# Late operands in their order of use, a pinned sum, and first loads behind a store, in a one-core encoder layer

## The chip, the cores and the metric

The kernel runs on one core of one Trainium2 chip. The metric is device time in microseconds (us): the median of several executions, with the lowest and the highest beside it. One more execution is taken with the hardware profiler; its page and its trace are what the views below show. Their times are microseconds from the start of its span.

The engines are called by their names in the profile: PE (TensorE, matmuls), ACT (ScalarE), DVE (VectorE), POOL (GpSimd) and SP (SyncE, which here only issues DMAs). An engine works through its own queue in order; a waiting instruction holds everything behind it.

## The reference, cut to what matters

One layer over 1024 positions with a width of 1024, all in f32:

```python
h = x
hn = rmsnorm(h, norm_mix_g)
z = hn @ w_in                       # pooling mixer and chunked attention
h = h + concat([pool_mixer(u), chunk_attention(q, k, v)]) @ w_out
hn = rmsnorm(h, norm_ffn_g)
up = hn @ w_up                      # 1024 -> 2 * 2816
gt, val = up[..., :2816], up[..., 2816:]
gt = causal_dwconv(gt, conv_w, conv_b)          # width 3 along the positions
h = h + (gelu(gt) * val) @ w_down   # the second projection, 2816 -> 1024
hn = rmsnorm(h, norm_ple_g)
gate = sigmoid(hn @ w_ple_gate + b_ple_gate)
h = h + gate * (p @ w_ple)          # p: 256 wide per position
return rmsnorm(h, final_g)
```

The change lies in the gated MLP (`w_up`, `w_down`) and in the passage to the embedding projection (`p @ w_ple`).

## The kernel before

**Split matmuls.** Every f32 operand is split into a high part (ACT rounds it, L133) and a low part (DVE subtracts, L134); the helper is `split`. `mm3` multiplies two split operands with three matmuls (L128 to L130). Where an operand is to be negated, ACT does so at L990 and DVE at L991.

**First projection.** The 2816 columns are 22 tiles `fi` of 128. Each tile is computed with seven products, numbered 1 to 7, after the manner of a fast 2x2 block scheme; `steps` gives their order, for tiles from 2 on (1, 5, 6, 2, 7, 3, 4). `up(fi, ...)` runs them. A product is 12 matmuls. Its weights are sums of blocks of `w_up`, which SP loads into a ring of six buffers `rawu` (`fetch`, L699), DVE adds (`summed`, L703) and `split` splits. Small steps take the results up: L788, L792 (ACT), L811, L812, L819, L822, L828 (DVE); the convolution and the GELU are L837 to L840; L854, L856 and L847 multiply gate and value.

**Second projection.** The results of tiles 0 to 19 are stored to DRAM (`Yd`, L898) and used in five groups of four tiles, again with seven products per group, here in the order (1, 2, 5, 4, 6, 7, 3) (`DOWN_ORDER`). They are called product 1 to 7 below, the ones of the first projection up products. Each is 24 matmuls and four additions to the result (`down_next`, L1008), placed between the up products of a later tile (`downs`, `places`). Its operands are sums of blocks of `w_down` and `Yd`: `ask` issues the first block's load on SP (L956) and the further ones as accumulating DMAs on POOL (L954) into the raw buffers `RW`. `split_next` splits them into four pairs, three of them in the tile `BQ`. In the last group product 4's activation operand is formed in part by DVE: at L986 it adds the buffer "grow", which holds product 5's operand, to the buffer "one".

**The end.** Tiles 20 and 21 do not go through DRAM. Their `w_down` blocks, the embedding `pT` and its weights `w_ple` are the late operands: twelve pieces, loaded on SP (L1068) into free `rawu` buffers named in `late` and split by `late_pairs`, in the order of `pieces`. Then come the embedding projection (`ple_mm`, 48 matmuls for the first half), the second projection of tiles 20 and 21 (`down_mm`), the gate and the last norm.

**What sets the order.** PE's order is that of the program (a manual schedule). The other engines' queues are set out at build time by a scheduler by priority, except for instructions marked with `keep_in_program_order` or `issue_after`. The marked ones of before are the twelve late pairs, the first split of the second projection and its first loads:

```python
def late_pairs(n):
    for _ in range(n):
        src, hi, lo = pieces[npiece[0]]
        t = late[npiece[0]]
        npiece[0] += 1
        sp.dma_start(t, src)
        split(t, hi, lo, True)
```

Of the kernel before, what the change touches and what calls it, by code (L numbers as in the profile page):

```python
# [9 lines left out]
ALU = mybir.AluOpType  # L10
# [83 lines left out]
def trunk(tc, xT, pT, vecs, w_qk0, w_in, w_v, bias, counts, pool_w, w_out, w_up, w_down,  # L94
          w_gate, w_ple, out):
    nc = tc.nc
    act, dve, pe, pool, sp = nc.scalar, nc.vector, nc.tensor, nc.gpsimd, nc.sync

    with tc.tile_pool(name="sb", bufs=1) as sb, \
# [20 lines left out]
        def f(kb, n):  # L120
            return F[:, int(kb * KW):int(kb * KW) + n]
# [206 lines left out]
        def keys(i):  # L328
            t = i % NTOK
            k0 = max(0, t - 4)  # L330
            return i // NTOK, t, k0, t + 1 - k0
# [209 lines left out]
        for i in range(NI + 3):  # L541
            if i < NI:
                h, t, k0, nk = keys(i)
# [40 lines left out]
        HS = [slice(0, 512), slice(512, 1024)]  # L584
# [3 lines left out]
        Yb = f(52.25, 1024)  # L588
# [82 lines left out]
        rawu = [f(2 * s, 512) for s in range(4)] + [f(40, 512), f(42, 512)]  # L671
# [83 lines left out]
        for z, d in enumerate((0, 4, 1, 5, 2, 6, 3, 7)):  # L755
            k = z // 2
# [33 lines left out]
        def seed(to, bank, scale=1.0):  # L790
            with tc.high_priority(AHEAD):
                act.activation(PS[:, to], PS[:, bank], AF.Copy, scale=scale)  # L792
# [34 lines left out]
        def gate0(bank):  # L827
            dve.tensor_tensor(Gb[:, 2:2 + 512], PS[:, bank], rst[:, HS[0]], ALU.mult)  # L828
# [13 lines left out]
        def values_in(ts, negative=None):  # L842
            b = max(ts.start, 512)
            if ts.stop > b:
                dve.tensor_tensor(V[:, b:ts.stop], V[:, b:ts.stop], rst[:, b:ts.stop], ALU.mult)
            if negative is None:
                dve.tensor_tensor(Yb[:, ts], Yb[:, ts], V[:, ts], ALU.mult)  # L847
                return
            for h in range(2):
                if HS[h].stop <= ts.start or HS[h].start >= ts.stop:  # L850
                    continue
                y = Yb[:, HS[h]]
                if h == negative:
                    dve.scalar_tensor_tensor(y, y, -1.0, V[:, HS[h]], ALU.mult, ALU.mult)  # L854
                else:
                    dve.tensor_tensor(y, y, V[:, HS[h]], ALU.mult)  # L856

        def store(dst, ts=slice(0, SEQ)):
            split(Yb[:, ts], dst[:, ts], dst[:, 1024 + ts.start:1024 + ts.stop])
# [13 lines left out]
        Yd = {fi: dp.tile([P, SEQ], F32, name=f"Yd{fi}") for fi in range(NF - 2)}  # L873
# [9 lines left out]
        def up(fi, dst, hooks=None):  # L883
            if fi == 0:
                pool.memset(Gb[:, 0:2], 0.0)
                gate0(firsts[0][0])
            if fi == 1:
                seed(firsts[1][1], firsts[1][0], -1.0)
            for n in steps[fi]:
                step(fi, n)  # L890
                for hook in (hooks or {}).get(n, ()):
                    hook()
            if isinstance(dst, int):

                for part in [HS[0:1], HS[1:2]] if fi == NF - 3 else [HS]:
                    values_in(slice(part[0].start, part[-1].stop), dst)
                    for ts in part:
                        sp.dma_start(Yd[fi][:, ts], Yb[:, ts])  # L898
                        stored.add((fi, HS.index(ts)))
                    ask()  # L900
                if fi > 3:
                    split_next()
                return
            for ts in HS if fi % 2 else [slice(0, SEQ)]:
                values_in(ts)
                if dst is not None:
                    store(dst, ts)

        stored = set()
        raws, pairs = {}, {}  # L910
        split_done, asked = set(), set()

# [18 lines left out]
        def buffer(side, n):  # L931
            return "grow" if n in (5, 6, 3) else "one"

        def ask(pinned=False):

            if not raws:
                return
            for side in "wa":
                for kind in ("one", "grow"):
                    queue = todo_of[side, kind]  # L940
                    while queue:
                        g, n, before = queue[0]
                        if before is not None and (side,) + before not in split_done:
                            break
                        if side == "a" and not all((group_of(g)[2 * k + j], t) in stored for k, t in parts(side, g, n)[0] for j in range(2)):
                            break
                        queue.pop(0)
                        asked.add((side, g, n))
                        grown = parts(side, g, n)[1]
                        for j, srcs in sources(side, g, n):  # L950
                            t = raws[side, kind, j]
                            for z, src in enumerate(srcs):
                                if z or grown:
                                    pool.dma_start(t, src, accum_op=ALU.add)  # L954
                                else:
                                    i = sp.dma_start(t, src)  # L956
                                    if pinned:
                                        tc.keep_in_program_order(i)

        todo_of = {}  # L960
        for side in "wa":
# [11 lines left out]
        def split_next(pinned=False):  # L973
            if nsplit[0] == len(sequence) or nsplit[0] > ndown[0]:
                return
            g, n = sequence[nsplit[0]]
            if not all((side, g, n) in asked for side in "wa"):
                return
            nsplit[0] += 1
            for side in "wa":  # L980
                sign = -1.0 if side == "a" and n in NEGATIVE else 1.0
                for j in range(2):
                    t = raws[side, buffer(side, n), j]
                    hi, lo = pairs[side, j]
                    if (side, g, n) == ("a", 4, 4):
                        dve.tensor_tensor(t, t, raws["a", "grow", j], ALU.add)  # L986
                    if sign > 0:
                        split(t, hi, lo, pinned)
                    else:
                        act.activation(hi, t, AF.Copy, scale=-1.0)  # L990
                        dve.scalar_tensor_tensor(lo, t, -1.0, rv(hi), ALU.mult, ALU.subtract)  # L991
                split_done.add((side, g, n))
            ask()
# [24 lines left out]
        for fi in range(4):  # L1018
            up(fi, negative(fi))
            if fi == 1:  # L1020
                b_pool = tc.tile_pool(name="bq", bufs=1)
                bp = b_pool.__enter__()
                B = bp.tile([P, 3072], F32R, name="BQ")
                RW = bp.tile([P, 4096], F32, name="RW")
                spots = [B[:, 1024 * z:1024 * (z + 1)] for z in range(3)] + [r(60, 1024)]
                for s, side in enumerate("wa"):
                    for j in range(2):
                        p_ = spots[2 * s + j]
                        pairs[side, j] = p_[:, 0:512], p_[:, 512:1024]
                        for q, kind in enumerate(("one", "grow")):  # L1030
                            z = 4 * s + 2 * q + j
                            raws[side, kind, j] = RW[:, 512 * z:512 * (z + 1)]
                ask(True)
            if fi == 2:
                for d in range(4):
                    for a, b, op in ((H[4 + d][:, HS[0]], H[4 + d][:, HS[1]], ALU.subtract),
                                     (H[d][:, HS[1]], H[4 + d][:, HS[1]], ALU.add)):
                        dve.tensor_tensor(a, a, b, op)
                ask()
                split_next(True)  # L1040
# [8 lines left out]
        wp = [(r(44 + 8 * k, 1024), r(48 + 8 * k, 1024)) for k in range(2)]  # L1049
        pt = [[(r(b, 512), r(b + 2, 512)) for b in (96 + 16 * h, 104 + 16 * h)] for h in range(2)]  # L1050
        banks = (4, 5, 6, 7, 0, 2, 1, 3)
        nl = len(loads)
        late = [rawu[(nl + z) % 6] for z in (0, 1, 5, 3, 2, 0, 1, 5, 3, 4, 2, 0)]
        pieces = []
        for z, fi in enumerate(last_f):
            pieces += [(w_down[fi, :, ts], wd2[z][0][:, ts], wd2[z][1][:, ts]) for ts in HS]
        pieces += [(pT[k, :, HS[0]], *pt[0][k]) for k in range(2)]
        for k in range(2):
            pieces += [(w_ple[k, :, ts], wp[k][0][:, ts], wp[k][1][:, ts]) for ts in HS]
        pieces += [(pT[k, :, HS[1]], *pt[1][k]) for k in range(2)]  # L1060
        npiece = [0]

# [8 lines left out]
        up(last_f[0], None, downs(last_f[0], (3, 5)))  # L1071
        hooks = downs(last_f[1], (0, 2, 4, 6))
        hooks.setdefault(1, []).insert(0, lambda: store(gv2[0]))
        for n, many in ((5, 2), (6, 4), (7, 4), (4, 2)):
            hooks.setdefault(n, []).insert(0, lambda many=many: late_pairs(many))
        up(last_f[1], gv2[1], hooks)
        b_pool.__exit__(None, None, None)
# [211 lines left out]
```

## Time and profile before

| what | before |
|---|---|
| median of 3 executions | 1149.34 us (1148.21 to 1151.45) |
| profiled execution | 1145.45 us |
| its span, first to last instruction | 1143.7 us |
| PE busy | 1127.9 us (99%) |
| DVE busy | 889.5 us (78%) |
| ACT busy | 604.6 us (53%) |
| POOL busy | 142.9 us (12%) |
| mean granted clock of PE | 0.996 |
| HBM read, written | 109.13 MB, 14.68 MB |

How to read the rows below: a timeline row gives start, duration, engine, line and operation, output and input, and, in brackets, how long the engine stood idle before it and what ended that. A row of the waits gives the waiting group, what released it, the total, how often, and the longest. A row of the chain of waits gives start, duration and what ran. A row of a window gives its length and, for PE, PEld, DVE, ACT and POOL, busy time and number of instructions, then the granted clock, the DMA share and GB/s. A row of DMA issues gives the median time from issue to landing at its end. PE matmuls overlap: what counts is from start to start, 0.227 us for one of 128x512 at full clock.

### The profile page before, as it was taken

What the parts mean: (1) busy time and instruction counts of PE and PEld (TensorE: products, weight loads), DVE (VectorE), ACT (ScalarE), POOL (GpSimd) and SP (SyncE); (2) the same over time, 40 slices, a digit from 0 to 9 for tenths busy, and PEclk for the clock granted to TensorE, in tenths of its full rate; (3) what the DMA queues carried; (4) which work ended last, traced back from release to release, by engine and by line L of the source; (5) the groups of instructions that cost most, each with busy time, mean ns of one, the idle gap of its engine ahead of it and who ended that gap; (6) DMA issues with size and microseconds to landing.
All of it is one profiled execution on the core that took longest, in us unless ns stands there. A gap on an engine that the chain in (4) does not pass through costs nothing.

```text
span 1143.7 us, 15749 instructions
## 1 busy us (share of the span) xinstructions
PE 1127.9 (99%) x5675; PEld 956.1 (84%) x5675; DVE 889.5 (78%) x1546; ACT 604.6 (53%) x1071; POOL 142.9 (12%) x188
## 2 busy tenths in 40 slices
PE   9999999999999999999999999999999999999997
PEld 7988998888888878888888888888888878788897
DVE  7678878879658788878788778877878779886864
ACT  8568677765655544434353435343534444574644
POOL 0000000073002200120112011201120112000000
PEclk9999999999999999999999999999999999999999
DMA  7110102104500244575558455745574547320012
GB/s 265 38 49 31 50 12 68 40 28 147 176 19 10 76 128 138 142 172 139 156 144 179 130 156 148 170 134 152 146 177 133 146 131 158 118 93 19 1 75 74
DMA packets 64446, 124.84 MB, mean 109 GB/s; under 512 B 7280, under 2 KB 8560, under 8 KB 64368
## 3 DMA queue, kind: packets, MB, share of 16 engines
q1 hardware_dynamic: 50400, 98.60, 25.4%
q0 software_dynamic: 13824, 25.17, 13.6%
q8 instruction: 44, 0.72, 0.3%
q14 instruction: 34, 0.28, 0.1%
q10 hardware_dynamic: 144, 0.07, 0.0%
HBM read 109.13 MB, written 14.68 MB: 108 GB/s over the span
## 4 chain that ended last, share of the span: by engine, by line
PE 88%; DVE 4%; issue 2%; ACT 2%; DMA 1%; POOL 1%; SPq 0%; DVEq 0%; POOLq 0%; ACTq 0%
PE PS L129 27%; PE PS L128 27%; PE PS L130 27%; PE PS L370 2%; DVE R L134 2%; PE PS L388 1%; PE PS L387 1%; PE PS L345 1%; PE PS L344 1%; ACT R L133 1%; DMA F<-in_w_down 1%; DMA F<-in_w_up 0%; DMA F<-in_w_qk 0%; PE PS L353 0%; PE PS L352 0%
## 5 line engine op out<-in xcount | busy, mean ns | idle before, releaser
L128 PE MATMUL PS<-R 128*128 128x512 f32 (+1 forms) x1176 | 442.2, 376 | 2.9 <-ACT PS L792 2.2
L130 PE MATMUL PS<-R 128*128 128x512 f32 (+1 forms) x1176 | 437.6, 372 | 0.0
L129 PE MATMUL PS<-R 128*128 128x512 f32 (+1 forms) x1112 | 419.8, 377 | 0.3 <-DVE R L233 0.3
L128 PEld LDWEIGHTS PS<-R 128*128 128x128 f32 x1176 | 221.6, 188 | 40.7 <-ACT PS L792 2.6
L130 PEld LDWEIGHTS PS<-R 128*128 128x128 f32 x1176 | 221.4, 188 | 38.8
L129 PEld LDWEIGHTS PS<-R 128*128 128x128 f32 x1112 | 209.4, 188 | 37.4 <-DVE R L233 1.3
L133 ACT ACTIVATE R<-F 128x512 fp32r<-128x512 f32 (+2 forms) x225 | 140.8, 637 | 178.7 <-PE PS L129 79.4
L134 DVE TENSOR_TENSOR R<-F,R 128x512 fp32r<-128x512 f32 (+2 forms) x221 | 152.4, 699 | 49.4 <-ACT R L133 48.0
L703 DVE TENSOR_TENSOR F<-F 128x512 f32<-128x512 f32 x88 | 60.5, 687 | 45.6 <-DMA F<-in_w_up 44.0
L1008 DVE TENSOR_TENSOR F<-F,PS 128x512 f32<-128x512 f32 x140 | 91.9, 679 | 3.8 <-PE PS L130 3.8
L133 ACT ACTIVATE BQ<-RW 128x512 fp32r<-128x512 f32 x90 | 52.4, 622 | 77.3 <-PE PS L129 77.3
L954 POOL DMA_DIRECT2D RW<-Yd x56 | 49.0, 876 | 256.4 <-DMA RW<-Yd 209.1
L954 POOL DMA_DIRECT2D RW<-in_w_down x40 | 35.9, 942 | 239.3 <-DMA RW<-in_w_down 192.8
L134 DVE TENSOR_TENSOR BQ<-RW,BQ 128x512 fp32r<-128x512 f32 x90 | 58.9, 683 | 1.1 <-ACT BQ L133 0.7
L129 PE MATMUL PS<-BQ 128*128 128x512 f32 x140 | 54.9, 392 | 3.1 <-DVE BQ L134 2.0
L837 ACT ACTIVATE F<-F,vec 128x1024 f32<-128x1024 f32 (+1 forms) x25 | 28.6, 1143 | 53.4 <-DVE F L812 49.7
L356 ACT ACTIVATE F<-F,small 128x640 f32<-128x640 f32 (+2 forms) x64 | 44.3, 693 | 21.3 <-DVE small L354 13.3
L129 PE MATMUL PS<-R,BQ 128*128 128x512 f32 x140 | 55.1, 393 | 0.2 <-DVE R L991 0.2
L128 PE MATMUL PS<-BQ 128*128 128x512 f32 x140 | 54.8, 392 | 0.2 <-ACT BQ L990 0.2
L128 PE MATMUL PS<-R,BQ 128*128 128x512 f32 x140 | 54.9, 392 | 0.0
L130 PE MATMUL PS<-R,BQ 128*128 128x512 f32 x140 | 54.8, 391 | 0.0
L130 PE MATMUL PS<-BQ 128*128 128x512 f32 x140 | 54.7, 391 | 0.0
(188 smaller groups left out, 1805.6 us busy)
## 6 DMA issues: line engine op xcount, KB each, us to landing
F<-in_w_up SPq DMA_DIRECT2D x91, 256.0 KB, 4.3
RW<-Yd SPq DMA_DIRECT2D x60, 256.0 KB, 3.6
RW<-Yd POOLq DMA_DIRECT2D x56, 256.0 KB, 5.0
RW<-in_w_down SPq DMA_DIRECT2D x50, 256.0 KB, 2.8
RW<-in_w_down POOLq DMA_DIRECT2D x40, 256.0 KB, 6.0
Yd<-F SPq DMA_DIRECT2D x40, 256.0 KB, 3.1
F<-in_w_in SPq DMA_DIRECT2D x10, 512.0 KB, 3.5
F<-in_xT SPq DMA_DIRECT2D x16, 256.0 KB, 5.8
```

The lines of the kernel that those rows point to most:

```text
L128: pe.matmul(ps, ahi, bhi, start=first, stop=False, skip_group_check=more)
L129: pe.matmul(ps, ahi, blo, start=False, stop=False, skip_group_check=more)
L130: pe.matmul(ps, alo, bhi, start=False, stop=last, skip_group_check=more)
L133: both = (act.activation(hi, src, AF.Copy), dve.tensor_tensor(lo, src, rv(hi), ALU.subtract))
L134: dve.tensor_tensor(lo, src, rv(hi), ALU.subtract))
L344: pe.matmul(PS[:, 4 + z, 0:320], q, K2[:, ks], start=True, stop=False)
L356: act.activation(S[:, 0:n], S[:, 0:n], AF.Exp, bias=s_[:, 0:1], scale=-1.0, accum_out=s_[:, 1:2])
L370: pe.transpose(pst[:, j * P:(j + 1) * P], S[:, j * P:(j + 1) * P], ident)
L703: dve.tensor_tensor(rawu[to], rawu[a], rawu[b], op)
L837: act.activation(y, Gb[:, 2 + a:2 + b], AF.Identity, bias=vec[:, C_CB + fi:C_CB + fi + 1], scale=cw(2))
L954: pool.dma_start(t, src, accum_op=ALU.add)
L1008: dve.tensor_tensor(t, t, PS[:, 4 + d], ALU.subtract if n in (1, 5) else ALU.add)
```

## The change

It has three parts. First, the first loads for the second projection, asked for when tile 1 is done, are no longer pinned in program order but issued behind the last store of tile 1's result. Second, the sum at L986 is kept in program order, which is behind the additions of product 5. Third, the late operands are asked for in the order in which the end uses them (embedding and its weights ahead of `w_down`), and later: 2 before product 6, 4 before product 7 and 6 before product 3, instead of 2 after up product 5, 4 before product 6, 4 before product 7 and 2 before product 3. The buffers in `late` follow.

```diff
-                        sp.dma_start(Yd[fi][:, ts], Yb[:, ts])
+                        written[0] = sp.dma_start(Yd[fi][:, ts], Yb[:, ts])
...
-        def ask(pinned=False):
+        def ask():
...
-                                    i = sp.dma_start(t, src)
-                                    if pinned:
-                                        tc.keep_in_program_order(i)
+                                    sp.dma_start(t, src)
...
                     if (side, g, n) == ("a", 4, 4):
-                        dve.tensor_tensor(t, t, raws["a", "grow", j], ALU.add)
+                        tc.keep_in_program_order(dve.tensor_tensor(t, t, raws["a", "grow", j], ALU.add))
...
-                ask(True)
+                with tc.issue_after(written[0].ins):
+                    ask()
...
-        late = [rawu[(nl + z) % 6] for z in (0, 1, 5, 3, 2, 0, 1, 5, 3, 4, 2, 0)]
-        pieces = []
+        late = [rawu[(nl + z) % 6] for z in (0, 1, 5, 3, 0, 1, 2, 4, 5, 3, 0, 1)]
+        pieces = [(pT[k, :, HS[0]], *pt[0][k]) for k in range(2)]
+        for k in range(2):
+            pieces += [(w_ple[k, :, ts], wp[k][0][:, ts], wp[k][1][:, ts]) for ts in HS]
         for z, fi in enumerate(last_f):
             pieces += [(w_down[fi, :, ts], wd2[z][0][:, ts], wd2[z][1][:, ts]) for ts in HS]
-        pieces += [(pT[k, :, HS[0]], *pt[0][k]) for k in range(2)]
-        for k in range(2):
-            pieces += [(w_ple[k, :, ts], wp[k][0][:, ts], wp[k][1][:, ts]) for ts in HS]
         pieces += [(pT[k, :, HS[1]], *pt[1][k]) for k in range(2)]
...
-        for n, many in ((5, 2), (6, 4), (7, 4), (4, 2)):
+        for n, many in ((6, 2), (7, 4), (4, 6)):
             hooks.setdefault(n, []).insert(0, lambda many=many: late_pairs(many))
```

More of the change, by code (lines that the diff above doesn't have):

```diff
@@ L907, in up @@
                     store(dst, ts)
-        stored = set()
+        stored, written = set(), [None]
         raws, pairs = {}, {}
```

## The prediction

> **What bounds the kernel now.** I read the page's busy line first, then the waits of TensorE alone, then the chain of waits and the timelines of the engines around each wait. All times are microseconds from the span's start, and lines are those of the kernel before.
>
> ```profile
> span 1143.7 us, 15749 instructions
> PE 1127.9 (99%) x5675; PEld 956.1 (84%) x5675; DVE 889.5 (78%) x1546; ACT 604.6 (53%) x1071; POOL 142.9 (12%) x188
> ```
>
> TensorE is busy for 1127.9 of 1143.7, so an edit that leaves its work alone can gain only where it pauses. The waits of TensorE have three entries that the three edits touch:
>
> ```profile
> PE PS L128 <- ACT PS L792: 2.2, 1, 2.2
> PE PS L129 <- DVE BQ L134: 2.0, 1, 2.0
> ...
> PE PS L129 <- DVE BQ L991: 1.1, 1, 1.1
> ```
>
> The profiled execution took 1145.45, its span 1143.7 and 1.75 around it. The median of the runs is 1149.34, 3.9 higher. I form the sum on the profiled execution and take it off the median. The changed kernel was built for its order of instructions: TensorE's order is the same to the last matmul, so only the other engines' queues move.
>
> **Edit one: first second-projection loads behind tile 1's store.** The chain of waits and the timelines of PE and VectorE (DVE) around the first wait:
>
> ```profile
> 393.07 0.42 SPq L956
> ...
> 393.60 5.21 DMA F<-in_w_up
> ...
> 398.90 0.70 DVE F L703
> ```
>
> ```profile
> 402.34 0.39 PE L130 MATMUL PS<-R 128*128 128x512 f32 x1
> 404.94 0.50 PE L128 MATMUL PS<-R 128*128 128x512 f32 x1 [2.20 <-ACT PS L792]
> 405.27 0.40 PE L129 MATMUL PS<-R 128*128 128x512 f32 x1
> ```
>
> ```profile
> 391.51 1.28 DVE L134 TENSOR_TENSOR R<-F,R 128x512 fp32r<-128x512 f32 x2
> ...
> 395.41 0.68 DVE L812 TENSOR_TENSOR F<-F 128x512 f32<-128x512 f32 x1
> ```
>
> ```profile
> DMA to landing us min/median/max: 2.4/2.7/5.2
> ```
>
> The last row is of the w_up loads (L699) up to 440. One of them is released when the two splits end at 391.51 + 1.28 = 392.8. Two w_down loads stand before it on SP's queue, so it goes at 393.60 and lands after 5.21, with their transfers beside it. VectorE stands still until 398.90, and the chain from there to TensorE's restart takes 404.94 - 398.90 = 6.04. In the new order nothing stands between: issue at 392.8, landing after 2.7 to 5.2, so 395.5 to 398.0. VectorE is free at 396.1, after L812. With the median landing the restart is possible at 396.1 + 6.04 = 402.1; TensorE would want it one matmul after 402.34, at 402.57. The wait goes, with 0.5 to spare; the second matmul of before came at 405.27 where 402.80 was due, so the gain is **2.5**. A landing of more than 3.7 leaves a piece, at 5.2 one of 1.5. I take 2.5, because the w_down transfers that lengthened the 5.21 are gone.
>
> What is moved comes later in a heap. In the new SP queue stand tile 1's stores, four w_down and four Yd loads, then the w_up loads for tiles 3 and 4; on POOL's queue two w_down additions (L954), issued at 398 so far, follow the loads as well. Nobody needs the second-projection data before 438. The w_up load for tile 3 may suffer:
>
> ```profile
> 426.09 1.28 SPq L956 DMA_DIRECT2D RW<-Yd  x3
> 428.26 0.81 SPq L699 DMA_DIRECT2D F<-in_w_up  x2
> ```
>
> ```profile
> 432.19 0.69 DVE L703 TENSOR_TENSOR F<-F 128x512 f32<-128x512 f32 x1 [1.13 <-DMA F<-in_w_up]
> ...
> 446.77 1.52 DVE L134 TENSOR_TENSOR R<-F,R 128x512 fp32r<-128x512 f32 x2
> ```
>
> ```profile
> 448.61 0.39 PE L128 MATMUL PS<-R 128*128 128x512 f32 x1
> ```
>
> ```profile
> F<-in_w_down SPq DMA_DIRECT2D x1, 256.0 KB, 6.9
> ```
>
> It was issued at 428.26, which is 425.8 once TensorE is 2.5 earlier. The second store, 2.5 earlier, goes at about 421.6; seven loads at 1.28 / 3 = 0.43 each and a wait of about 1 for the store's own landing put the w_up load at about 426.3. L703 would start at 429.7; the new order sets two operations (0.6 each) and their waits ahead of it, so it can start at about 431.7. The load has 5.4 to land: it took 432.19 - 428.26 = 3.9 before, and the longest SP load of this trace took 6.9 (issued at 966.97, among many). At 6.9 VectorE is 1.5 late, and the next thing due is the split that starts at 446.77, ends 0.68 later and feeds the product at 448.61, 1.1 later. So the cost is 0 to 0.4. I take 0, as 3.9 is the nearer row.
>
> **Edit two: the sum for product 4 (L986) pinned behind product 5's additions.**
>
> ```profile
> 935.97 0.69 DVE L986 TENSOR_TENSOR RW<-RW 128x512 f32<-128x512 f32 x1 [5.61 <-DMA RW<-Yd]
> ```
>
> ```profile
> 940.94 0.39 PE L128 MATMUL PS<-BQ 128*128 128x512 f32 x1
> 943.31 0.50 PE L129 MATMUL PS<-BQ 128*128 128x512 f32 x1 [1.98 <-DVE BQ L134]
> ...
> 955.70 0.39 PE L128 MATMUL PS<-BQ 128*128 128x512 f32 x1
> ...
> 956.60 0.39 PE L129 MATMUL PS<-R,BQ 128*128 128x512 f32 x1
> 956.83 0.39 PE L130 MATMUL PS<-R,BQ 128*128 128x512 f32 x1
> ```
>
> ```profile
> 400.00:406.00 6.00, 3.80 (x18) 2.80 (x17) 6.00 (x9) 3.07 (x5) 0.13 (x1) 1.00 0.64 129
> ```
>
> ```profile
> 943.00:945.00 2.00, 1.69 (x5) 1.43 (x6) 2.00 (x4) 0.00 (x0) 1.77 (x2) 0.74 0.75 109
> ```
>
> VectorE's queue blocked for 5.61 on a sum that nobody needed yet; product 5's operands came late, and product 5, which began at 940.94, paused 1.98. Product 5 (24 matmuls), tile 20's last product and tile 21's first (12 each) are 48 x 0.227 = 10.9, so product 4 was due at 951.84 and began at 955.70: 3.86 lost. The pause is 1.98 of it; the rest, 1.9, is restart and a stretch at a lower granted clock (0.74 on average from 943 to 945).
>
> In the new order product 5's operands are ready before 940.94. But the two sums now stand late, and the queue has other work before and between them. From the end of tile 20's product 3 (941.1) VectorE runs ten operations of 512, and two of 1024. Their prices:
>
> ```profile
> 951.10 1.28 DVE L839 SCALAR_TENSOR_TENSOR F<-F,vec 128x1024 f32<-128x1024 f32 x1
> ...
> 955.30 0.68 DVE L991 SCALAR_TENSOR_TENSOR R<-RW,R 128x512 fp32r<-128x512 f32 x1
> 955.90 0.68 DVE L822 TENSOR_TENSOR V<-PS,F 128x512 f32<-128x512 f32 x1
> ...
> 957.70 1.22 DVE L847 TENSOR_TENSOR F<-F,V 128x1024 f32<-128x1024 f32 x1
> ```
>
> ```profile
> 951.18 0.61 ACT L990 ACTIVATE R<-RW 128x512 fp32r<-128x512 f32 x1
> ```
>
> One of 512 takes 955.90 - 955.30 = 0.60 of the queue, one of 1024 1.2. That is 6.0 + 2.4, to 949.5. A split follows that waits for tile 20's product 4 (TensorE ends it at 940.94 + 36 x 0.227 = 949.1) and ScalarE's half of it (0.6): it starts at 949.8. Then come seven of 0.60 (that split, first sum, L822, L703, first L991, split, second sum), to 954.0; ScalarE's L990 (0.61) is hidden under L847 (1.15); the last L991 (0.68) ends at 955.8. Product 4's fifth matmul needs it. It would run at 955.85 and the sixth, after a restart of 0.34 as at 404.94, at 956.2, against 956.83 before. So of the 3.86 only **0.6** comes back: product 4 waits instead of product 5, about 2.5 in three pieces (first L991, second L990, second L991).
>
> Whether a slow stretch follows is open. After the pause of 1.98 it did; after the one of 2.20 the clock stayed at 1.00 in the window from 400 to 406. The price is 0 or, by subtraction above, 1.7. I take half, 0.85, since one of two pauses of this length paid it. [...]
>
> **Edit three: late operands in the order of use.**
>
> ```profile
> 973.85 0.63 ACT L133 ACTIVATE R<-F 128x512 fp32r<-128x512 f32 x1 [5.60 <-DMA F<-in_w_down]
> ```
>
> ```profile
> 977.23 0.39 PE L130 MATMUL PS<-R 128*128 128x512 f32 x1
> ...
> 979.49 0.50 PE L129 MATMUL PS<-BQ 128*128 128x512 f32 x1 [1.14 <-DVE BQ L991]
> ...
> 981.27 0.40 PE L128 MATMUL PS<-BQ 128*128 128x512 f32 x1
> ```
>
> ScalarE stood 5.60 on a pinned late pair while product 7's operands lay behind it. 981.27 is product 7's seventh matmul, due at 977.23 + 7 x 0.227 = 978.8: 2.45 lost. In the new order only the two p pairs stand before product 7; they were issued in the places of 927 and 938 and have long landed. Product 7's operands are then ready some 2.6 before it begins: **2.45** back. Ten pairs now come later, four after product 7's operands and six after the last up product, each 0.6 on VectorE and less on ScalarE. TensorE runs product 7 from 976.9 to 982.3, the last two up products to 987.8, product 3 to 993.2 and 48 matmuls of the embedding projection to 1004.1. VectorE has product 7's operands at 974.1, six operations with two waits for TensorE to 978.6, the four pairs to 981.0, four additions to 983.4 and product 3's operands to 985.8, which is 2.0 ahead of its start. After the last up product come eight operations and the six pairs, to 996, 8 ahead of the first use of w_down. The loads of these pairs wait on SP for buffers that earlier splits free between 964 and 981; with 6.9 to land they are there before the pairs' turn, at 978 and 992. Without that cover six pairs would cost 3.6.
>
> Sum: 2.5 + 0.6 + 2.45 - 0.85 = 4.7. The forecast is 1149.34 - 4.7 = **1144.6**; the profile by the same sum 1140.8.
>
> **The rivals.** *Half given back*: after product 4's wait the full slow stretch (1.7), 0.4 at tile 3, and 0.6 of the first wait stays, with a landing of 4.3. Then 5.55 - 2.7 = 2.85: 1146.5. For it speaks that product 4's pause is longer than either quoted one; against it that the heaped loads are issued 5.4 ahead of need.
>
> *No slow stretch*: the pause comes in three pieces, and after wait three, also in pieces, matmuls went on undisturbed: 1149.34 - 5.55 = 1143.8.
>
> *No wait at product 4*: the 5.61 that VectorE stood still turn into a lead that reaches product 4, and all of 3.86 comes back: 5.55 + 3.25 = 8.8, so 1140.5. Against it speak the operations between the sums.
>
> *Slower*: product 6's operand is added by POOL into the buffer that the pinned sum reads.
>
> ```profile
> 946.16 0.86 POOL L954 DMA_DIRECT2D RW<-Yd  x1 [1.33 <-DVE V L845]
> ```
>
> ```profile
> RW<-in_w_down POOLq DMA_DIRECT2D x2, 256.0 KB, 7.4
> ```
>
> That addition went at 946.16; behind the second sum it goes at about 954.5, after two w_down additions on POOL's queue. Product 6 is due 48 matmuls after 955.70, at 966.6, now 0.6 earlier; its fifth matmul, at 966.9, needs the data 0.61 + 0.68 before, at 965.6. The slowest POOL transfers shown took 7.4, which ends at 962; from 11 on each microsecond costs one, and beyond 15.8 the kernel is slower than before. If it came to 18, 1151.5.
>
> **How the numbers follow.** About 0.3% (3.4) is what a measurement of this kernel can tell from no change. Chances: forecast 0.50, own range 1143.2 to 1146.0; half given back 0.22; no stretch 0.11; no wait at product 4 0.08; slower 0.09. Faster by over 0.3% means below 1145.9: nearly all of the forecast's share, the two better rivals and a little of the first: 0.67. Within 0.3%: 0.24. Slower: 0.09. The range leaves out the best and the slower rival, and allows about 1.5 for the medians: 1141.8 to 1148.2.
>
> **What would show it.** Right: the waits of TensorE lose L792, L134 and the three around 978; a new group on L991 and L990 (renumbered) stands at product 4, some 2.5 in all; the L986 rows wait for no DMA; L703 near 396 has no DMA wait; the ScalarE row with 5.60 is gone. Wrong: TensorE waits between 440 and 450 in tile 3, at product 6, or in the embedding projection; or no wait at product 4.

## The result and the profile after

| | before | after |
|---|---|---|
| median, in the comparison of the two | 1147.86 us (7 runs, 1146.09 to 1151.45) | 1143.73 us (7 runs, 1141.33 to 1145.58) |
| ratio, 95% interval | | 0.996 [0.9943, 0.9977] |
| profiled execution | 1145.45 us | 1145.58 us |
| its span | 1143.7 us | 1143.8 us |

The changed kernel is faster by 4.1 us by the medians, by 4.6 by the ratio (0.004 of 1147.86); 4.7 were forecast. The two profiled executions are as long as each other all the same: the one of before is shorter than any of the seven runs beside it, the one of after the longest of its own. The traces show where waits went; what a step is worth has to come from medians. A second trace of the changed kernel, from the experiments below, took 1141.86.

The busy line of the page of after, and its waits of TensorE:

```profile
span 1143.8 us, 15743 instructions
PE 1129.3 (99%) x5675; PEld 957.4 (84%) x5675; DVE 890.4 (78%) x1546; ACT 604.6 (53%) x1071; POOL 143.1 (13%) x188
```

```profile
PE PS L128 <- ACT R L988: 1.1, 1, 1.1
PE PS L128 <- ACT PS L792: 1.0, 1, 1.0
...
PE PS L129 <- DVE BQ L989: 0.6, 1, 0.6
PE PS L128 <- ACT BQ L988: 0.4, 1, 0.4
PE PS L128 <- ACT R L133: 0.3, 1, 0.3
...
PE PS L129 <- DVE R L989: 0.3, 1, 0.3
```

The groups of before, L792 with 2.2, L134 with 2.0 and L991 with 1.1, are gone. (L986, L990 and L991 are now L984, L988 and L989.) The L792 that stands here is another wait, in tile 3. The four entries on L988 and L989 are product 4's; the timeline of PE shows them, and what follows:

```profile
952.56 0.50 PE L128 MATMUL PS<-BQ 128*128 128x512 f32 x1 [0.41 <-ACT BQ L988]
953.70 0.51 PE L129 MATMUL PS<-BQ 128*128 128x512 f32 x1 [0.64 <-DVE BQ L989]
955.57 0.79 PE L128 MATMUL PS<-R,BQ 128*128 128x512 f32 x1 [1.14 <-ACT R L988]
956.64 0.79 PE L129 MATMUL PS<-R,BQ 128*128 128x512 f32 x1 [0.28 <-DVE R L989]
957.23 0.63 PE L130 MATMUL PS<-R,BQ 128*128 128x512 f32 x1
957.66 0.63 PE L128 MATMUL PS<-BQ 128*128 128x512 f32 x1
```

The pauses add up to 2.47. After them matmuls follow each other at 957.66 - 957.23 = 0.43 instead of 0.227. The stages by windows (length; busy time of PE, PEld, DVE, ACT, POOL; granted clock):

```profile
435.00:452.00 17.00, 15.74 (x68) 12.08 (x67) 15.81 (x24) 9.84 (x16) 0.88 (x1) 1.00 0.66 178
938.00:946.00 8.00, 8.00 (x37) 6.64 (x36) 7.96 (x14) 3.10 (x5) 1.76 (x2) 1.00 0.44 69
954.00:962.00 8.00, 6.58 (x16) 4.53 (x15) 5.62 (x8) 1.69 (x2) 2.65 (x4) 0.57 0.97 203
970.00:990.00 20.00, 20.00 (x90) 16.57 (x89) 18.58 (x30) 10.35 (x19) 0.00 (x0) 1.00 0.52 157
990.00:1120.00 130.00, 130.00 (x720) 113.66 (x719) 96.19 (x157) 74.14 (x124) 3.16 (x3) 1.00 0.15 49
```

Product 5's wait (in 938 to 946) and wait three (in 970 to 990) are gone, and the embedding projection waits for nothing. From 954 to 962 the granted clock is 0.57: in finer windows it is at half from about 955.0, for 6.83. In tile 3 TensorE stands idle for 17.00 - 15.74 = 1.26. Before, tile 3 lost nothing, and the lower clock lasted 3.41.

### The profile page after: what moved, and what is told of

The parts are those of the page before. It is cut to its first block, busy times and chain, and to the rows that moved or that the text cites. A ratio compares the mean times of both kernels' runs of the same rounds, so it can differ in the third digit from the quotient of the medians.

```text
span 1143.8 us, 15743 instructions
## 1 busy us (share of the span) xinstructions
PE 1129.3 (99%) x5675; PEld 957.4 (84%) x5675; DVE 890.4 (78%) x1546; ACT 604.6 (53%) x1071; POOL 143.1 (13%) x188
## 4 chain that ended last, share of the span: by engine, by line
PE 87%; DVE 6%; issue 2%; ACT 2%; DMA 2%; POOL 1%; SPq 0%; DVEq 0%; POOLq 0%; ACTq 0%
PE PS L129 26%; PE PS L128 26%; PE PS L130 26%; PE PS L370 2%; DVE R L134 2%; PE PS L388 1%; PE PS L387 1%; PE PS L345 1%; PE PS L344 1%; DMA F<-in_w_up 1%; ACT R L133 1%; DMA F<-in_w_qk 1%; PE PS L353 0%; PE PS L352 0%; DVE F L703 0%
## 5 line engine op out<-in xcount | busy, mean ns | idle before, releaser
L134 DVE TENSOR_TENSOR R<-F,R 128x512 fp32r<-128x512 f32 (+2 forms) x221 | 152.7, 700 | 55.2 <-ACT R L133 54.3
L703 DVE TENSOR_TENSOR F<-F 128x512 f32<-128x512 f32 x88 | 60.6, 688 | 41.0 <-DMA F<-in_w_up 39.2
L134 DVE TENSOR_TENSOR BQ<-RW,BQ 128x512 fp32r<-128x512 f32 x90 | 59.1, 686 | 2.5 <-PE PS L129 1.3
L612 ACT ACTIVATE F<-F 128x512 f32<-128x512 f32 (+1 forms) x49 | 27.9, 570 | 45.5 <-DVE F L1154 16.7
```

The lines of the kernel that those rows point to most:

```text
L134: dve.tensor_tensor(lo, src, rv(hi), ALU.subtract))
L612: act.activation(self.q, src, AF.Square)
L703: dve.tensor_tensor(rawu[to], rawu[a], rawu[b], op)
```

## The experiments

**Each edit alone.** Three kernels, each the kernel before with one of the edits. Together they tell whether the edits' effects add up, and which of them carries the gain.

```diff
 first alone:                -                ask(True)
                             +                with tc.issue_after(written[0].ins):
                             +                    ask()
 second alone:               +                        tc.keep_in_program_order(dve.tensor_tensor(t, t, raws["a", "grow", j], ALU.add))
 third alone:                late and pieces in the new order, and
                             +        for n, many in ((6, 2), (7, 4), (4, 6)):
```

> Only the first edit: the first second-projection loads behind tile 1's store; sum and late operands as before. Theory A (each edit takes its own wait away and makes a smaller one elsewhere): TensorE's wait on L792 at 405 (2.2 us) is gone, and a wait of 0.9 to 1.3 us on ScalarE appears near 440 in tile 3, because the w_up load of tile 3 is issued behind eight loads and takes over 7 us to land. The waits of product 5 (about 2.0) and product 7 (1.1 + 0.2 + 0.2) stay. Net 0 to 1.5 us below before. Rival B (the wait in tile 3 of the changed kernel comes from another edit): no wait near 440, net 2.5 to 4 us below before.

> Only the second edit: the sum for product 4 pinned behind product 5's additions. Theory A: product 5's wait (2.0 us) is gone and product 4 waits instead, in three or four pieces, 2.3 to 2.8 us in all, on L990 and L991; wait one and wait three stay. Net between 1.5 us below and 1.5 us above before, depending on the slow-clock stretch that follows. Rival B (product 4's wait in the changed kernel comes from the new places of the late pairs, which also stand in VectorE's queue there): no wait at product 4, net 3.5 to 5 us below before.

> Only the third edit: late operands in order of use and later. Theory A: the ScalarE wait of 5.6 us on a w_down load and TensorE's waits at product 7 (1.6 us idle, 2.45 lost) are gone, the waits on L792 and at product 5 stay, no new wait in the embedding projection: 2 to 3.5 us below before. Rival B (VectorE is so full at the end that the six pairs moved there cost what is gained): a new TensorE wait between 985 and 1010, net under 1 us.

| edit alone | median | ratio to before (1148.09), 95% interval | us |
|---|---|---|---|
| first loads | 1145.3 | 0.9981 [0.997, 0.9992] | -2.2 |
| sum pinned | 1149.32 | 1.0015 [1.0004, 1.0026] | +1.7 |
| late operands | 1144.87 | 0.9973 [0.9962, 0.9984] | -3.1 |

The last column is the ratio's difference from 1, times the median of before, and so are the gains of the runs further on. They sum up to -3.6; the whole gave -4.6, and -5.2 when it was run again (below). Each of the three is known to about 1.3, so this does not show whether the edits add up exactly. The middle edit alone makes the kernel slower, and the other two carry the gain. The waits of TensorE with the first edit alone have no L792 at all, neither near 404 nor in tile 3, where theory A expected one, and its -2.2 lies between the ranges of the two theories; in the timeline its product 5 and product 7 still wait:

```profile
940.86 0.50 PE L129 MATMUL PS<-BQ 128*128 128x512 f32 x1 [1.46 <-DVE BQ L134]
...
977.42 0.50 PE L129 MATMUL PS<-BQ 128*128 128x512 f32 x1 [1.15 <-DVE BQ L991]
```

With the second edit alone, product 5's wait is gone and product 4 waits in the same four pieces as in after, 2.85 in all, with a window at granted clock 0.80 behind them; its +1.7 is 0.2 above the expected range:

```profile
954.50 0.50 PE L128 MATMUL PS<-BQ 128*128 128x512 f32 x1 [0.49 <-ACT BQ L990]
955.64 0.50 PE L129 MATMUL PS<-BQ 128*128 128x512 f32 x1 [0.64 <-DVE BQ L991]
...
957.51 0.50 PE L128 MATMUL PS<-R,BQ 128*128 128x512 f32 x1 [1.15 <-ACT R L990]
958.58 0.63 PE L129 MATMUL PS<-R,BQ 128*128 128x512 f32 x1 [0.57 <-DVE R L991]
```

```profile
954.00:962.00 8.00, 5.15 (x14) 3.30 (x13) 6.87 (x10) 3.14 (x5) 3.53 (x4) 0.80 0.86 171
```

**The sum early.** If product 4 waits because the pinned sums stand too late on VectorE, then they belong directly behind the last of product 5's splits: late enough not to block them, early enough for product 4. The edit on the changed kernel:

```diff
-                        tc.keep_in_program_order(dve.tensor_tensor(t, t, raws["a", "grow", j], ALU.add))
+                        with tc.issue_after(last_lo[0].ins):
+                            dve.tensor_tensor(t, t, raws["a", "grow", j], ALU.add)
...
-                        split(t, hi, lo, pinned)
+                        i = split(t, hi, lo, pinned)
+                        if (g, n) == (4, 5):
+                            last_lo[0] = i
```

It was run twice, in two comparisons; the changed kernel itself was run again in a third.

> The changed kernel, with the two sums for product 4 placed right behind the last split of product 5's operands (issue_after) instead of behind product 5's additions. Theory A (product 4 waits only because the sums and what the queue put between them stand too late): the sums run near 940 and 941.5, product 4's operands are ready before it begins, TensorE has no wait between 945 and 965 and no slow-clock stretch there; 3 to 5 us below the changed kernel, so 7 to 9 us below before. The tile 3 wait near 440 stays. Rival B (VectorE is simply short of time there, in whatever order): product 4 still waits over 1.5 us, time within 1.5 us of the changed kernel.

> The changed kernel with the early sum once more, beside the two others that have it. Theory A (its gain over the changed kernel is the pause at product 4 and the half-clock stretch behind it): 1137.5 to 1139.5, one wait of about 1.0 at product 4, mean granted clock 0.997 to 0.999. Rival B (a lucky chip): 1140 to 1143.

> The changed kernel once more, beside the others on one chip. Theory A (tile 3's wait hangs on how long one w_up load takes to land, and that differs from run to run; product 4's pause and the half-clock stretch behind it come every time): 1142 to 1146; product 4 waits 2.0 to 2.7 in three or four pieces and the granted clock from 954 to 962 is 0.5 to 0.85; tile 3 waits anything from 0 to 1.3. Rival B (tile 3's wait belongs to the changed order and comes every time): the wait on L792 near 442 again, 0.9 to 1.3, with a landing over 6.

| | median | ratio to before, 95% interval | granted clock, mean of the runs |
|---|---|---|---|
| changed kernel again | 1143.35 (9 runs) | 0.9955 [0.9939, 0.9971] | 0.9956 |
| with the early sum | 1138.55 (5 runs) | 0.9921 [0.9907, 0.9934] | 0.9978 |
| with the early sum, again | 1138.03 (6 runs) | 0.9917 [0.9896, 0.9938] | 0.9983 |

In its first trace the early sums stand at 938.24 and 940.05 on VectorE's timeline, where after has them at 951.16 and 954.16, and product 4 has one wait, where none was expected; in its second trace it has none at all, and one of 1.0 was expected. Neither trace waits in tile 3, though the first expectation had that wait stay:

```profile
938.24 0.68 DVE L986 TENSOR_TENSOR RW<-RW 128x512 f32<-128x512 f32 x1
...
940.05 0.68 DVE L986 TENSOR_TENSOR RW<-RW 128x512 f32<-128x512 f32 x1
```

```profile
950.98 0.50 PE L129 MATMUL PS<-BQ 128*128 128x512 f32 x1 [1.00 <-DVE BQ L993]
```

No window of either trace from 930 to 1000 has a clock below 1.00. The gain over the changed kernel is 4.8 to 5.3 by the medians (1143.35 - 1138.55 and 1143.35 - 1138.03) and 3.9 to 4.4 by the ratios; two kernels below that were run side by side and differ in this edit alone lie 5.5 apart. About 2.9 of it is clock, by an estimate. That is worked out from the runs' mean granted clock, since a time T at a mean clock c holds T x (1 - c) of loss: 1143 x 0.0045 = 5.1 for the changed kernel, 1138 x 0.0019 = 2.2 with the early sum. The rest fits the pauses at product 4, 2.3 to 2.5 in the traces of the changed kernel against 0 to 1.0.

**The early sum without the other edits.** The same edit on the kernel before.

> The kernel before with one edit: the sum for product 4 stands behind the last split of product 5's operands, not behind product 5's additions in program order. The other two edits are left out. Theory A (edit two removed a wait and made another by standing too late): product 5's wait is gone, product 4 waits about 1.0 once, no half-clock stretch there, 1143 to 1145.5. Rival B (the late sum was not what cost; the waits around product 4 come from VectorE being full): product 4 waits 2 or more again, 1147 to 1150.

It took 1146.43, ratio 0.9982 [0.9968, 0.9997], so -2.1, where the sum in program order costs 1.7: 3.8 lie between two places of the same two additions. The time is 0.9 above the expected range, though product 4 waits for only 0.17. Its trace has wait three with 0.53 and 1.67, and this time a lower clock behind it:

```profile
970.00:990.00 20.00, 17.81 (x70) 13.73 (x69) 18.77 (x31) 11.23 (x20) 0.00 (x0) 0.91 0.35 117
```

**Order or lateness of the late operands.** The third edit does two things. One kernel takes only the hooks and the buffers (asked for later, `w_down` first as before), the other only the order of the pieces (asked for as early as before).

```diff
 later only:
-        for n, many in ((5, 2), (6, 4), (7, 4), (4, 2)):
+        for n, many in ((6, 2), (7, 4), (4, 6)):
 order only:
+        pieces = [(pT[k, :, HS[0]], *pt[0][k]) for k in range(2)]
...
```

> The kernel before with the late operands asked for later (2 before product 6, 4 before product 7, 6 before product 3), but in the old order, w_down first. Theory A (what blocked product 7 was the number of pinned pairs ahead of its operands; the order matters only for the end): the waits on L990 and L991 around 978 go, and the embedding projection, whose operands now come last, waits 0.5 to 3.6 near 993; 1145 to 1148.5. Rival B (the order makes the gain): product 7 waits as before, 1147 to 1149.5.

> The kernel before with the late operands in the new order (embedding and its weights ahead of w_down), but asked for as early as before: 2 after up product 5, 4 before product 6, 4 before product 7, 2 before product 3. Theory A (what blocks product 7 is that ten pairs stand ahead of its operands, in whatever order): product 7 waits as before, 2.0 to 2.6 lost near 978, 1147 to 1149.5. Rival B (the order does a part): that wait shrinks and the time is 1144.5 to 1146.5.

Later only took 1144.95, ratio 0.9973 [0.996, 0.9987]: -3.1, the gain of the whole edit. Wait three is gone, and the embedding projection waits no more than 0.1, so what theory A added, a wait of 0.5 to 3.6 at the end, did not come. Order only took 1150.23, ratio 1.0017 [1.0003, 1.003]. In that kernel the embedding's operands are written so early that the last tile still works in their buffers, and part of what it computes is another; its time and its waits are what is read here. Its TensorE does not wait near 978, as theory A had it, but earlier, in the up product before, for splits of both engines; ScalarE then stands 6.11, until TensorE has left a buffer, and the clock is at half for 6.83, from 968.36 on:

```profile
967.28 0.49 PE L128 MATMUL PS<-R 128*128 128x512 f32 x1 [1.21 <-ACT R L133]
969.90 0.79 PE L129 MATMUL PS<-R 128*128 128x512 f32 x1 [2.12 <-DVE R L134]
```

```profile
974.63 0.63 ACT L133 ACTIVATE R<-F 128x512 fp32r<-128x512 f32 x1 [6.11 <-PE PS L129]
```

So lateness (with its buffers) alone makes the gain; the new order adds nothing that these medians show. What the order alone would cost is left open, since that kernel differs in more than the order.

**The heap ahead of tile 3's load.** Two kernels move the first second-projection loads elsewhere. One asks for them behind the last `w_up` load issued so far; it was run with and without the early sum. The other, with the early sum, asks for them in tile 2, after its product 6, so that tile 3's first loads go ahead of them.

```diff
 earlier:                    +                with tc.issue_after(last_up[0].ins):
 behind tile 3's loads:      +            up(fi, negative(fi), {steps[2][3]: [heap]} if fi == 2 else None)
```

> The changed kernel with the first second-projection loads behind the last w_up load issued so far, not behind tile 1's store: tile 3's w_up load then stands ahead of most of the heap. Theory A (tile 3's wait is the load that stands behind the heap): no wait in tile 3, and up to 2.0 faster than the changed kernel where that has the wait, 1142 to 1144.5. Rival B (the w_down transfers lie beside w_up loads again and lengthen them): the wait on L792 near 404 comes back with 0.5 to 2.2, and the time is 1144 to 1147.

> The changed kernel with both: the sum for product 4 behind the last split of product 5's operands, and the first loads behind the last w_up load. Theory A (the two costs are separate): 1136.5 to 1138.6, nothing in tile 3, one wait of about 1.0 at product 4, no half-clock stretch. Rival B (the early loads cost what they save): 1139 to 1141.

> The changed kernel with the early sum, and with the first second-projection loads behind tile 3's first w_up loads on SP's queue (asked for after product 6 of tile 2). Theory A (the heap ahead of that load is what made it late): L704 near 432 waits for no load or starts by 430.5, nothing in tile 3, 1136.5 to 1138.5, the spread of the runs no wider than 2. Rival B (the heap comes too late for the first splits of the second projection, near 438): a wait of TensorE of 0.5 to 2 between 438 and 455, 1139 to 1141.

| | median | ratio to before, 95% interval |
|---|---|---|
| earlier | 1144.03 | 0.9967 [0.9953, 0.9981] |
| earlier, with the early sum | 1138.53 | 0.9916 [0.9896, 0.9937] |
| behind tile 3's loads, with the early sum | 1138.1 | 0.9911 [0.9893, 0.993] |

The earlier loads helped nothing. TensorE does not wait near 404, as rival B had it, but it waits in tile 3 after all: 1.58 in the first kernel, and 1.00 with the early sum, whose expectation had nothing there (and one wait at product 4, where there is none). SP's timeline says why: two `Yd` loads still stand ahead of tile 3's `w_up` loads, and wait for the store of tile 1 to land. A row of SP's waits and one of VectorE's timeline follow it.

```profile
420.24 1.52 SPq L898 DMA_DIRECT2D Yd<-F  x2
422.09 0.80 SPq L699 DMA_DIRECT2D F<-in_w_up  x1
426.39 0.80 SPq L956 DMA_DIRECT2D RW<-Yd  x2
427.28 1.74 SPq L699 DMA_DIRECT2D F<-in_w_up  x3
```

```profile
SPq L956 <- DMA Yd<-F: 3.4, 1, 3.4
```

```profile
433.15 0.69 DVE L703 TENSOR_TENSOR F<-F 128x512 f32<-128x512 f32 x1 [4.49 <-DMA F<-in_w_up]
```

In the third kernel tile 3's first loads go from 422.17 on, L704 (the L703 of the others) starts at 428.71 without a wait, and tile 3 has no wait either; yet its median is that of the early sum without it, 1138.1 against 1138.03. So the heap makes the load late, as the prediction feared, but on the median of the runs it costs nothing that can be measured.

## Why the prediction was right, point by point

TensorE runs the same 5675 matmuls in the same order in every kernel here, so its starts can be compared one by one. The table has, for a stretch of before between two matmul starts, how much longer (+) or shorter (-) the same stretch is in another trace:

| stretch of before | forecast | after | second trace of after | with the one edit alone | with the early sum (two traces) |
|---|---|---|---|---|---|
| 402.34 to 440.00, the first wait | -2.5 | -2.52 | -2.52 | -2.52 (first) | -2.52, -2.52 |
| 440.00 to 459.94, tile 3 | 0 | +2.13 | +0.19 | +0.49 (first) | +0.09, 0.00 |
| 940.94 to 964.99, products 5 and 4 | +0.25 (0.85 - 0.6) | +2.43 | +0.98 | +1.69 (second) | -2.54, -3.79 |
| 964.99 to 989.90, product 7 | -2.45 | -2.47 | -2.47 | -2.47 (third) | -2.47, -2.47 |

Two of the four terms came out to 0.02, in every trace that has the edit. The other two were too small: tile 3 in one trace of two, and the pinned sum, with what follows it, in all three. (Before's own stretch at products 5 and 4 already holds 3.41 at half clock.)

**The first wait, 2.5: right.** The wait near 404 is gone, and VectorE goes from L812 to L703 without standing still:

```profile
395.99 0.69 DVE L812 TENSOR_TENSOR F<-F 128x512 f32<-128x512 f32 x1
396.59 1.41 DVE L703 TENSOR_TENSOR F<-F 128x512 f32<-128x512 f32 x2
```

The edit alone brought 2.2. The three loads of `w_up` issued from 391 to 396 land after 2.6 by the median, where the one of before took 5.21, and no piece of the wait stays.

**Tile 3, 0 with a bound of 0.4: its bound was too low.** The issue was forecast at about 426.3 (the terms as written, 421.6 + 7 x 0.43 + 1, make 425.6) and came at 427.10, in the second trace at 426.38. The landing was mis-sized, with 3.9 taken and 6.9 as the bound; the chain of waits and the timelines of VectorE, ScalarE and TensorE in after show:

```profile
427.10 7.71 DMA F<-in_w_up
```

```profile
434.83 0.69 DVE L703 TENSOR_TENSOR F<-F 128x512 f32<-128x512 f32 x1 [2.56 <-DMA F<-in_w_up]
435.64 0.63 ACT L133 ACTIVATE R<-F 128x512 fp32r<-128x512 f32 x1 [4.21 <-DVE F L703]
442.35 0.50 PE L128 MATMUL PS<-R 128*128 128x512 f32 x1 [0.96 <-ACT PS L792]
```

TensorE stood idle for 1.26, and with the restarts 2.13 were lost. The prediction looked for the loss at one place only, the split that feeds the product at 448.61. But ScalarE waits for the same L703, here for 4.21; its L792, further back in its queue, then holds TensorE at 442.35, some 6 earlier. In the second trace of the same kernel VectorE had the data 2.4 earlier, at 432.41, and TensorE lost 0.19; the first edit alone and both traces of the early sum lost 0 to 0.5. The value 0 was near for most traces, and the bound wrong for one.

**The pinned sum, 0.6: the mechanism was right.** The forecast put the last L991 at 955.8 (its end), product 4's wait at about 2.5 in three pieces, and product 5's wait at none. The trace has product 5 without a wait, 2.47 in four pieces, and that operation from 955.90 to 956.58, 0.8 later than forecast, of which 0.2 is that product 5 starts at 941.11 there and at 940.94 before:

```profile
954.16 0.69 DVE L984 TENSOR_TENSOR RW<-RW 128x512 f32<-128x512 f32 x1
954.77 1.22 DVE L847 TENSOR_TENSOR F<-F,V 128x1024 f32<-128x1024 f32 x1
955.90 0.68 DVE L989 SCALAR_TENSOR_TENSOR R<-RW,R 128x512 fp32r<-128x512 f32 x1
```

**The stretch at a lower clock, 0.85: too small.** Product 4's pauses brought 6.83 at half clock in the first trace (3.4 lost), 3.41 in the second (1.7), 3.41 with the second edit alone (1.7) and nothing where the loads were moved earlier: 1.7 on average of these four, the end of the range 0 to 1.7 and not its middle. By the runs' clocks it is up to 2.9. With 1.7 in its place the second edit would lose 1.1 where the forecast had it lose 0.25; 1.7 [0.5, 3.0] were measured.

The longest pause of TensorE in the 14 traces is 2.93 (order only), and no half clock follows it; stretches at half clock follow pauses from 1.67 on. Where finer windows were taken, each such stretch lasted 3.41, or 6.83 (the first trace of the changed kernel, and order only). The last section lists the pauses.

**Wait three, 2.45: right in size, with the cause half right.** The stage from 970 to 990 is full, and the edit alone brought 3.1, as the lateness alone did. The prediction counted which pairs stand ahead of product 7's operands, which is what mattered; which data these pairs carry did not. The cover that it named for the moved pairs, the work up to the embedding projection, held with the old order too.

**The rivals.** *No wait at product 4* fell with the four pieces. *Slower* fell too: the POOL addition was forecast at about 954.5 and went at 956.23, and TensorE waited for nothing at product 6.

```profile
956.23 0.88 POOL L954 DMA_DIRECT2D RW<-Yd  x1 [1.32 <-ACT R L988]
```

*Half given back* comes nearest to after's own trace, though by more at tile 3 and at product 4 and by nothing at the first wait. *No slow stretch* is seen only in the kernel with earlier loads; both traces of the changed kernel have a stretch, and the mean clock of each of its 16 runs is 0.995 or 0.996, against 0.997 to 0.999 with the early sum.

**The base.** The 4.7 were taken off a median of three runs, 1149.34, which later came out at 1147.86 to 1148.36. Off these the forecast would have been 1143.2 to 1143.7, against 1143.73 and 1143.35. In the forecast time two errors partly cancel, which is luck: a median that was 1 to 1.5 high, and a clock loss taken too small. Nor do the traces add up to the gain of the medians: the table's four steps make -0.4 in after and -3.8 in its second trace. They are measured against one trace of before, shorter than the seven runs beside it, and what the removed waits are worth in a median run no single trace says: product 5's wait, 1.98 there, was 1.46, 1.71, 2.82 and 2.93 in the four other kernels that leave its operands and the sum as they were. The gain is not clock: the mean clock of the runs is 0.9957 to 0.9958 before and 0.9954 to 0.9956 after.

## What to carry to other kernels

An operation that blocks an in-order queue (the sum held VectorE's for 5.61 in before) has two bad places, too early and too late: work out when its own consumer needs it, and tie it to the last instruction that must go ahead of it, not to "behind everything". Here that turned +1.7 into -2.1 alone, and -4.6 to -5.2 into -9.1 to -9.5 with the other edits. When operands block a queue, asking for them later can be the whole gain; and where the pauses of the matrix engine are near 2 us, compare medians and mean clocks before trusting one trace.

## What the runs showed of the hardware

Whether a pause was followed by half clock did not go by its length alone. There are 13 single pauses of 1.67 to 2.93 in the 14 traces, from 400 to 460 and from 930 to 1000. Those of 1.67 (the early sum without the other edits; an equal one, with the second edit alone, was not), 1.81 (third edit alone), 1.98 (before) and 2.06 (second edit alone) were followed by it; in one of 2.12 (order only), with one of 1.21 shortly before, it began 0.6 after the pause did; eight were not followed, among them 2.20 (before), 2.82 (later only) and 2.93 (order only). Of four pauses broken into pieces at product 4 (2.3 to 2.9 in all) three were, of two such at product 7 (1.6 in before, 2.3 with the first edit alone) none. Pauses up to 1.58 standing alone never were.

So nearly equal waits on one line differed in what they cost. The one on L792 near 405 was 2.06 with the second edit alone, and by windows of 0.5 the clock was at half from 405.84 to 409.25, for 3.41, which costs 1.7; in before it was 2.20, and no half clock followed. At product 4 a pause of 2.35 in pieces (earlier loads) was followed by none, those of 2.31 (second trace of after) and 2.85 (second edit alone) by 3.41, and that of 2.47 (after) by 6.83, which costs 3.4. What decides this is not shown here.

A 256 KB load of `w_up`, issued behind the same heap of second-projection loads at 426.31 (first edit alone), 426.38 (second trace of after) and 426.52 (first trace of the early sum), brought VectorE its data at 432.74, 432.41 and 432.44; issued at 427.10 in after, at 434.83. For the four `w_up` loads issued between 422 and 432 the median from issue to landing was 8.1 in after and 2.7 where three of them go ahead of the heap.
